# A hybrid mLSTM, attention and MLP layer on one core: another grouping of one weight preparation, block sums of the second MLP product made earlier, some stores on another queue

## The chip, the cores and the metric

The kernel runs on one core of a Trainium2 chip. The metric is the device time of one execution in microseconds (us). Its five engines are named as in the profile: PE (TensorE, matmuls; PEld is its weight load), DVE (VectorE), ACT (ScalarE), POOL (GpSimd) and SP (SyncE, which here does nothing but issue DMAs). Each engine works through its own list of instructions in order; an engine that waits at one instruction holds back all that stand behind it in its list.

## The reference

One layer, sequence 1024, width 1024, all in float32:

```
u    = rms_norm(h, norm1_g);  proj = u @ w_in
h    = h + concat(mlstm_mixer(proj...), neighbourhood_attention(proj...)) @ w_out
z    = rms_norm(h, norm2_g) @ w_ff1                 # 1024 x 4096
h    = h + square(relu(z)) @ w_ff2                  # 4096 x 1024
gate = sigmoid(rms_norm(h, ple_norm_g) @ w_ple_gate)
h    = h + gate * (p @ w_ple_up)
```

The change touches the third and fourth line alone, the MLP with its squared ReLU.

## The kernel before, in words

A float32 product is made of three passes: each operand x is split into a rounded part xh (ACT copies x into the type fp32r) and a rest xl = x - xh (DVE subtracts), and PE adds ah·bh, ah·bl and al·bh into one PSUM bank. So every block of weights costs an ACT copy, then a DVE subtraction, before PE can finish with it; in tile names the last letter, h or l, is that part. One matmul is 128x128 by 128x512.

**First MLP product (w_ff1).** The 4096 hidden columns are 16 groups of 256. Groups 2 to 15 are done by the Strassen-Winograd scheme, seven products of blocks instead of eight. Its products are called by their weight operands: 11, 12, 21, 22 are blocks of the weights, and s1 = 21 + 22, s2 = s1 - 11, s3 = 11 - 21, s4 = 12 - s2 are sums of them. `prep(c)` (with `put`) loads a group's weights, makes the sums and splits them into four pairs of tiles called a (11, 12), b (s2, s4), c (s3, 22) and d (s1); these tiles come from one ring with two buffers, so that c takes over the buffer of a, and d that of b, when PE has read it for the last time. The activations' sums (bt and the like) are made by `sum_blocks`. Group 2 is the first of its kind: `first_prods` runs its products while the activations' sums are still being made, with s2, s3 and 22 interleaved and s1 last. Groups 0 and 1 are plain products (p0a, p1a and, later, p0b, p1b), split in halves of which the first stand before group 2 and the second behind group 15.

While group 2 is on PE, `squares` sums h² over the width for the norm: ACT squares a 128x512 half (sq), POOL adds it to Rb; 14 adds, with two buffers for sq, so that the third square has to wait for the first add, and so on.

**The planes of z.** `relu2` and `z_blocks` make the squared ReLU's Winograd sums of a group's output and `z_put` stores them to DRAM as zd[0] to zd[3]; four halves go by SP's queue (`PQ`), the others by ACT's.

**Second MLP product (w_ff2).** `ff2_sweep` runs four sweeps, i = 2, 0, 1, 3, each with its own operands. A step of sweeps 2, 0 and 1 handles one group c with 24 matmuls (f_P): it needs zh and zl (the plane zr loaded and split, `zload`) and two blocks of w_ff2 (`w2_blocks`). In sweep 0 these blocks are sums: `w2_blocks(0, c)` loads ev (named w2re) and od (w2ro), 512 KB each, makes four sums (two on DVE, two on POOL), keeps two of them (sk) for sweep 1, and splits the other two, half by half, into w2h and w2l. `nadd` is how many of the former sweep's results are added to h (h<-h,evP) in a step.

**Order.** What stands ahead on an engine is set by the program's order and by `issue_after`, which ties a load to an earlier instruction; a step's loads and splits are issued some instructions ahead of its matmuls.

Of the kernel before, what the change touches and what calls it, by code (L numbers as in the profile page):

```python
# [18 lines left out]
P = 128  # L19
# [40 lines left out]
def tile_block(ctx, tc, xT, pT, w_in, w_out, w_ff1, w_ff2, w_gate, w_up, vecs, gate_b, rpbp, con,  # L60
# [95 lines left out]
    def wview(w, k0, k1, c0, c1):  # L156
        return w[k0 * P : k1 * P, c0:c1].rearrange("(k p) n -> p k n", p=P)
# [764 lines left out]
    with tc.tile_pool(name="m2", bufs=2) as m2, tc.tile_pool(name="m2p", bufs=2, space=PSUM) as m2p:  # L922
# [269 lines left out]
    with tc.tile_pool(name="ff1", bufs=1) as ff1:  # L1192
# [62 lines left out]
        def plain(nm, w, B1_, B2_, order, z):  # L1255
# [9 lines left out]
            for f in range(len(w)):  # L1265
                S.activation(z[f], pss[f], AF.Copy)

        def first_prods(nm, w, z):

            c11, c12, c21, u2 = z[0][:, 0:512], z[0][:, 512:], z[1][:, 0:512], z[1][:, 512:]  # L1270
            names = (("11", "11"), ("12", "21"), ("s4", "22"), ("s2", "t2"), ("s3", "t3"), ("22", "t4"), ("s1", "t1"))
            ps = {an: ps_(f"{nm}_{an}_{bn}") for an, bn in names}

            def part(an, bn, j):
                for i, (x_, y_) in enumerate(passes(w[an][0][:, j], w[an][1][:, j], *B[bn, j])):
                    TE.matmul(ps[an], x_, y_, start=j == 0 and i == 0, stop=j == 3 and i == 2)
# [16 lines left out]
            add(c12, c12, ps["s1"])  # L1293
            add(u2, u2, ps["s1"])
# [13 lines left out]
        def w2raw(i, c, rows, e0, e1, pool, tag, bufs):  # L1308
            raw = pool.tile([P, T], F32, tag=tag, name=f"w2r{i}_{c}", bufs=bufs)
            n = e1 - e0  # L1310
            for s, f in enumerate(rows):
                nc.sync.dma_start(raw[:, s * n : (s + 1) * n], w_ff2[f * P : (f + 1) * P, e0:e1])
            return raw

        def w2_blocks(i, c):

            wr = wp, "wr", 3
            if i == 0:
                ev = w2raw("e", c, (2 * c,), 0, D, ff2, "gh", 4)
                od = w2raw("o", c, (2 * c + 1,), 0, D, ff2, "gl", 4)  # L1320
                a11, a21, a12, a22 = ev[:, 0:512], ev[:, 512:], od[:, 0:512], od[:, 512:]
                sk[c] = utile32(f"sk{c}")
                s1, s3 = sk[c][:, 0:512], sk[c][:, 512:]
                V.tensor_tensor(s1, a21, a22, op=ALU.add)
                V.tensor_tensor(s3, a11, a21, op=ALU.subtract)  # L1325
                G.tensor_tensor(a21, s1, a11, op=ALU.subtract)  # L1326
                G.tensor_tensor(a22, a12, a21, op=ALU.subtract)
                hl = wp.tile([P, T], F32R, tag="wh", name=f"w2h0_{c}"), wp.tile([P, T], F32R, tag="wl", name=f"w2l0_{c}")
                for s, src in enumerate((a22, a21)):
                    ss = slice(s * 512, (s + 1) * 512)  # L1330
                    S.activation(hl[0][:, ss], src, AF.Copy)
                    V.tensor_tensor(hl[1][:, ss], src, hl[0][:, ss].bitcast(F32), op=ALU.subtract)
# [82 lines left out]
        wp1 = [plain_w("w1p", f, (utile(f"w1ph{f}"), utile(f"w1pl{f}"))) for f in (2, 3)]  # L1415
        sum_blocks(2)
        first_half(1, wp1)
        with after("t1"):
            w = prep(2)
        sum_blocks(3)  # L1420
        zt[2] = utile32("z2_0"), utile32("z2_1")
        first_prods("p2", w, zt[2])
# [53 lines left out]


    with tc.tile_pool(name="ff2", bufs=2) as ff2:
        acc3 = {}


# [58 lines left out]
        def g_split(j, t=None):  # L1540

            if j not in GH:
                GH[j] = (ff2.tile([P, T], F32R, tag="gh", name=f"gh{j}", bufs=4) if j < 4 else utile(f"gh{j}")), utile(f"gl{j}")
            hs = slice(0, T) if t is None else slice(t * 512, (t + 1) * 512)
            hi, lo = (t_[:, hs] for t_ in GH[j])
            g = vcol(V_G3, j)
            S.activation(hi, hres[j][:, hs], AF.Copy, scale=g)
            V.scalar_tensor_tensor(lo, hres[j][:, hs], g, hi.bitcast(F32), op0=ALU.mult, op1=ALU.subtract)
# [156 lines left out]
```

## Time and profile before

| | |
|---|---|
| time, median of 3 runs (lowest to highest) | 1400.39 us (1400.2 to 1402.23) |
| the profiled execution's own time | 1407.04 us |
| its span | 1405.3 us |
| PE busy | 1330.1 us, 95%, 7139 matmuls |
| PEld busy | 1109.6 us, 79% |
| DVE busy | 903.2 us, 64% |
| ACT busy | 598.5 us, 43% |
| POOL busy | 513.6 us, 37% |
| DMA | 211.27 MB, 150 GB/s in the mean |

PE is busy nearly throughout, so what can be won lies where it stops, or runs at less than its full clock. The share of the whole span tells little of that: a stop is read from the stage in which it stands. A line of a timeline gives the start, the duration, the engine, the line, out<-in, the shape, how many alike are merged, and in brackets how long the engine was idle before and who released it. Ends of matmuls are modelled, so their starts are what to compare.

### The profile page before, as it was taken

To read this page: it belongs to the slowest core of one execution; us is meant where nothing else is said; L and a number is where in the kernel's file an instruction comes from. 1 tells how busy PE (TensorE), PEld (TensorE's weight loads), DVE (VectorE), ACT (ScalarE), POOL (GpSimd) and SP (SyncE) were. 2 spreads that over 40 slices of the span, in tenths; PEclk is the share of its full clock that TensorE was granted. 3 is DMA by queue.
4 is the path that set the end of the run, shared out by engine and by line. 5 is a ranking of instruction groups with operands and counts; after the bars stand their busy time and mean duration, and the time that the engine had idled before them with its cause. 6 is when DMAs were issued, how large, how long until landed. Compare 5 with 4: busy or idle time off the path is not lost.

```text
span 1405.3 us, 19398 instructions
## 1 busy us (share of the span) xinstructions
PE 1330.1 (95%) x7139; PEld 1109.6 (79%) x7139; DVE 903.2 (64%) x1419; ACT 598.5 (43%) x985; POOL 513.6 (37%) x409
## 2 busy tenths in 40 slices
PE   7999999999998889999799999998999899999998
PEld 5988778799896667777587778886888678888887
DVE  4487786665672555667666666665448998559543
ACT  7353433364553545535433333334344234455321
POOL 2215675463321111100527665563302561007422
PEclk9999999999998899999899999999999999999999
DMA  8543333475323653313124644447786683542342
GB/s 291 197 147 96 107 108 106 169 228 165 109 65 102 177 162 126 105 61 103 45 85 163 220 155 149 145 135 239 268 300 212 196 254 102 167 148 74 106 142 83
DMA packets 158158, 211.27 MB, mean 150 GB/s; under 512 B 17904, under 2 KB 106992, under 8 KB 158064
## 3 DMA queue, kind: packets, MB, share of 16 engines
q1 hardware_dynamic: 149968, 192.07, 42.9%
q10 hardware_dynamic: 6624, 12.06, 2.5%
q0 software_dynamic: 1472, 5.92, 1.3%
q8 instruction: 56, 0.92, 0.3%
q14 instruction: 38, 0.31, 0.1%
HBM read 155.79 MB, written 54.21 MB: 149 GB/s over the span
## 4 chain that ended last, share of the span: by engine, by line
PE 56%; DVE 5%; DMA 5%; POOL 3%; issue 3%; ACT 2%; SPq 0%; DVEq 0%; POOLq 0%; ACTq 0%
PE f_P L1508 18%; PE op L1025 6%; PE p_s_t L256 6%; PE g L1577 6%; PE p L256 4%; PE p_s L256 2%; PE p_t L256 2%; DMA nr<-qnd 2%; PE pv L997 1%; PE pt L977 1%; PE o1p L312 1%; DMA tab<-tabI 1%; POOL Rb L1247 1%; PE p1a L1263 1%; PE sc L947 1%
## 5 line engine op out<-in xcount | busy, mean ns | idle before, releaser
L1345 DVE TENSOR_TENSOR zl<-zr,zh 128x1024 fp32r<-128x1024 f32 x56 | 81.9, 1470 | 20.1 <-ACT zh L1344 14.7
L966 POOL TENSOR_SCALAR pc<-pc,st 128x288 f32<-128x288 f32 (+1 forms) x32 | 17.4, 545 | 159.5 <-DVE st L961 124.8
L1344 ACT ACTIVATE zh<-zr 128x1024 fp32r<-128x1024 f32 x56 | 58.2, 1047 | 19.7 <-DMA zr<-zd 14.9
L1326 POOL TENSOR_TENSOR w2re<-sk,w2re 128x512 f32<-128x512 f32 x16 | 27.0, 1686 | 99.9 <-DVE sk L1325 85.2
L956 ACT ACTIVATE pc<-pc,st 128x288 f32<-128x288 f32 (+1 forms) x64 | 36.3, 569 | 56.0 <-DVE st L955 56.0
L1508 PE MATMUL f_P<-zl,w2h 128*128 128x512 f32 x128 | 52.3, 408 | 6.4 <-DVE zl L1345 6.4
L955 DVE CUSTOM_DVE_ANT_1 pc<-sc,tab 128x288 f32<-128x288 f32 (+1 forms) x64 | 29.9, 504 | 40.6 <-DMA tab<-tabU 22.0
L1508 PE MATMUL f_P<-zh,w2h 128*128 128x512 f32 x128 | 51.0, 398 | 1.1 <-ACT zh L1344 1.1
L1577 PE MATMUL g<-gh,wg_h 128*128 128x512 f32 (+1 forms) x136 | 51.8, 381 | 0.0
L1577 PE MATMUL g<-gl,wg_h 128*128 128x512 f32 (+1 forms) x136 | 51.3, 377 | 0.0
L1577 PE MATMUL g<-gh,wg_l 128*128 128x512 f32 (+1 forms) x136 | 51.2, 377 | 0.0
L1508 PE MATMUL f_P<-zh,w2l 128*128 128x512 f32 x128 | 51.1, 399 | 0.0
L790 POOL TENSOR_SCALAR wv<-vh,wj 128x129 f32<-128x129 f32 x56 | 30.4, 546 | 56.5 <-PE num L791 51.7
L1531 POOL TENSOR_TENSOR h<-h,evP 128x512 f32<-128x512 f32 x8 | 14.8, 1886 | 98.3 <-ACT evP L1522 98.3
L1372 POOL TENSOR_TENSOR tz<-z,z 128x512 f32<-128x512 f32 x14 | 19.4, 1388 | 73.2 <-ACT z L1358 73.1
L260 DVE TENSOR_TENSOR z<-z,p_s_t 128x512 f32<-128x512 f32 x52 | 34.5, 684 | 17.5 <-PE p_s_t L256 16.2
L1247 POOL TENSOR_TENSOR Rb<-Rb,sq 128x512 f32<-128x512 f32 x14 | 17.7, 1310 | 70.6 <-ACT sq L1245 70.6
L1357 DVE SCALAR_TENSOR_TENSOR z<-z,Rb 128x1024 f32<-128x1024 f32 x28 | 42.0, 1510 | 0.0
L997 PE MATMUL pv<-pT,vw 128*64 128x128 f32 (+1 forms) x384 | 32.2, 296 | 7.6 <-DVE pT L986 3.5
L1583 DVE TENSOR_TENSOR z<-g,Rb 128x512 f32<-128x512 f32 (+1 forms) x17 | 11.0, 658 | 43.4 <-PE g L1577 37.5
L138 ACT ACTIVATE w_bh<-w_0r 128x1024 fp32r<-128x1024 f32 x14 | 14.8, 1061 | 56.3 <-POOL w_0r L234 53.9
L138 ACT ACTIVATE w_ah<-w_0r 128x1024 fp32r<-128x1024 f32 x14 | 14.9, 1062 | 54.8 <-PE p_t L256 46.7
(840 smaller groups left out, 4782.9 us busy)
## 6 DMA issues: line engine op xcount, KB each, us to landing
zr<-zd SPq DMA_DIRECT2D x56, 512.0 KB
w2r<-w_ff SPq DMA_DIRECT2D x48, 256.0 KB
zd<-z ACTq DMA_DIRECT2D x42, 256.0 KB
zd<-tz SPq DMA_DIRECT2D x32, 256.0 KB
w2re<-w_ff SPq DMA_DIRECT2D x16, 512.0 KB
w2ro<-w_ff SPq DMA_DIRECT2D x16, 512.0 KB
w_0r<-w_ff SPq DMA_DIRECT2D x14, 512.0 KB
w_1r<-w_ff SPq DMA_DIRECT2D x14, 512.0 KB
```

The source lines that it names most:

```text
L256: TE.matmul(ps, x_, y_, start=j == 0 and i == 0, stop=j == 3 and i == 2)
L260: mark["add"] = V.tensor_tensor(o, a, b, op=ALU.add).ins
L790: G.tensor_scalar(wv, vh[:, c, 0:129], wj[:, col], 1.0, op0=ALU.mult, op1=ALU.mult)
L956: S.activation(pb, pb, AF.Exp, scale=-1.0, bias=st[:, 0:1], accum_out=st[:, 1:2])
L997: TE.matmul(pv[e0 : e0 + 64, cb], vws[pr][: 4 * kw, cb, rb + j, e0 : e0 + 64], pT[s][: 4 * kw, j], start=j == 0, stop=j == 2)
L1025: TE.matmul(ps, a, b, start=n == 0 and i == 0, stop=n == len(ks) - 1 and i == 2)
L1247: G.tensor_tensor(Rb[:, hs], Rb[:, hs], sq[:, hs], op=ALU.add)
L1344: S.activation(hi, raw, AF.Copy)
L1345: dv.append(V.tensor_tensor(lo, raw, hi.bitcast(F32), op=ALU.subtract).ins)
L1357: V.scalar_tensor_tensor(z_, z_, 0.0, Rb, op0=ALU.max, op1=ALU.mult)
L1508: pe_last = TE.matmul(ps[n, e], a, b, start=st and k == 0, stop=sp and k == 2)
L1577: TE.matmul(ps, x_, y_, start=k == 0 and i == 0, stop=k == KT - 1 and i == 2)
```

## The change

Three parts, all in the MLP.

1. `first_w()` takes the place of `prep(2)`. The same two loads, the same four sums; the blocks are grouped as a (11, 12), b (s4), c (s2, s3), d (22, s1), and each block is split by itself (512 columns). The tie of group 2's preparation to the activations' sums (`after("t1")`) goes.
2. `w2_load` and `w2_sums` take loads and sums out of `w2_blocks(0, c)`. All four sums are on DVE; they are made five groups ahead and the loads six (those of groups 0 to 4 during sweep 2, by the table `ahead`); two results overwrite the two halves of w2re, so that step c splits one tile of 1024 columns. w2re has six buffers and w2ro two, instead of four and four. Sweep 0's `nadd` is 1 instead of 2.
3. `z_put`: for c = 0, 1 and 15 the four stores of SP's queue are issued by POOL.

The diff, without the comment-free rest of `early`, whose tiles take buffers of the new rings:

```diff
+        def first_w():
+            raw = []
...
+            def put(x_, *parts):
+                hi, lo = (wp.tile([P, T], F32R, tag="w" + y_, name=f"w1_2_{x_}{y_}") for y_ in "hl")
+                for i, (an, src) in enumerate(parts):
+                    h_, l_ = hi[:, i * 512 : i * 512 + 512], lo[:, i * 512 : i * 512 + 512]
+                    S.activation(h_, src, AF.Copy)
+                    V.tensor_tensor(l_, src, h_.bitcast(F32), op=ALU.subtract)
+                    w[an] = [y_.rearrange("p (k n) -> p k n", n=P) for y_ in (h_, l_)]
+            put("a", ("11", a11), ("12", a12))
+            V.tensor_tensor(s1, a21, a22, op=ALU.add)
+            V.tensor_tensor(a21, a11, a21, op=ALU.subtract)
+            V.tensor_tensor(a11, s1, a11, op=ALU.subtract)
+            V.tensor_tensor(a12, a12, a11, op=ALU.subtract)
+            put("b", ("s4", a12))
+            put("c", ("s2", a11), ("s3", a21))
+            put("d", ("22", a22), ("s1", s1))
...
+        def w2_load(c):
+            w2eo[c] = w2raw("e", c, (2 * c,), 0, D, ff2p[0], "gh", 6), w2raw("o", c, (2 * c + 1,), 0, D, ff2p[0], "gl", 2)
+        def w2_sums(c):
+            ev, od = w2eo.pop(c)
...
+            V.tensor_tensor(s1, a21, a22, op=ALU.add)
+            V.tensor_tensor(s3, a11, a21, op=ALU.subtract)
+            V.tensor_tensor(a21, s1, a11, op=ALU.subtract)
+            V.tensor_tensor(a11, a12, a21, op=ALU.subtract)
+            skw[c] = ev
...
-                G.tensor_tensor(a21, s1, a11, op=ALU.subtract)
-                G.tensor_tensor(a22, a12, a21, op=ALU.subtract)
...
+                hl = split(wp, skw.pop(c), T, "w", f"w2_0_{c}")
+                for f_, c_ in ((w2_sums, c + 5), (w2_load, c + 6)):
+                    if c_ < NC_:
+                        f_(c_)
...
-            (PQ if (i, s) in ((0, 1), (1, 1), (1, 0), (3, 0)) else nc.scalar).dma_start(zd[i][:, c, s * 512 : (s + 1) * 512], src)
+            ((nc.gpsimd if c in (0, 1, NC_ - 1) else PQ) if (i, s) in ((0, 1), (1, 1), (1, 0), (3, 0)) else nc.scalar).dma_start(zd[i][:, c, s * 512 : (s + 1) * 512], src)
...
-        with after("t1"):
-            w = prep(2)
+        w = first_w()
...
+        ahead = {6 + 2 * c: [(w2_sums, c), (w2_load, c + 2)][: 2 if c < 4 else 1] for c in range(5)}
+        ahead[5] = [(w2_load, 0), (w2_load, 1)]
-        op, _ = ff2_sweep(2, 0, ("P2", "P1"), pre, {}, 0)
-        op, _ = ff2_sweep(0, 1, ("P3", "P6"), op, {}, 2)
+        op, _ = ff2_sweep(2, 0, ("P2", "P1"), pre, ahead, 0)
+        op, _ = ff2_sweep(0, 1, ("P3", "P6"), op, {}, 1)
```

PE's own order is that of before, but for the tiles that hold s2 and 22 of group 2. Where other engines' orders move, in three places:

ACT during group 2's products, before: the squares, then d (s1), then group 3's first weights.

```order
L1287 ACTIVATE z_1_6917<-p_11_11_6918 128x512
L1245 ACTIVATE sq_7042<-h_4888 128x512 x2
L1245 ACTIVATE sq_7042<-h_4943 128x512 x2
L1245 ACTIVATE sq_7042<-h_4998 128x512 x2
L1245 ACTIVATE sq_7042<-h_5137 128x512 x2
L1245 ACTIVATE sq_7042<-h_5196 128x512 x2
L1245 ACTIVATE sq_7042<-h_6546 128x512 x2
L138 ACTIVATE w_2_dh<-s_2_6874 128x512
L1245 ACTIVATE sq_7042<-h_6548 128x512
L138 ACTIVATE w_3_ah<-w_3_0r 128x1024
L1245 ACTIVATE sq_7042<-h_6548 128x512
```

The same place now (c is s2 and s3, d is 22 and s1):

```order
L1283 ACTIVATE w_2_ch<-w_2_0r 128x512
L1283 ACTIVATE w_2_ch<-w_2_1r 128x512
L1245 ACTIVATE sq_7048<-h_4888 128x512 x2
L1283 ACTIVATE w_2_dh<-w_2_1r 128x512
L1283 ACTIVATE w_2_dh<-s_2_6878 128x512
L1245 ACTIVATE sq_7048<-h_4943 128x512 x2
L1245 ACTIVATE sq_7048<-h_4998 128x512 x2
L1245 ACTIVATE sq_7048<-h_5137 128x512 x2
L1245 ACTIVATE sq_7048<-h_5196 128x512 x2
L1245 ACTIVATE sq_7048<-h_6546 128x512 x2
L1245 ACTIVATE sq_7048<-h_6548 128x512
L138 ACTIVATE w_3_ah<-w_3_0r 128x1024
```

Both copies of w_2_d have moved ahead of the squares that wait for POOL; w_3_ah stands where it stood, behind the last square but one.

SP's queue around the start of the second product (sweep 2's first two loads are zr_0 and zr_1; the four stores between them are group 15's), before:

```order
L1343 DMA zr_0_8973<-zd_108 128x1024
L1365 DMA zd_106<-tz_8963 128x512
L1365 DMA zd_107<-tz_8963 128x512
L1365 DMA zd_107<-z_0_8832 128x512
L1365 DMA zd_109<-z_1_8833 128x512
L1343 DMA zr_1_8986<-zd_108 128x1024
L1312 DMA w2r_2_9086<-w_ff 128x512
```

Now:

```order
L1382 DMA zr_0_8979<-zd_108 128x1024
L1341 DMA w2r_2_9092<-w_ff 128x512
L1382 DMA zr_1_8992<-zd_108 128x1024
L1474 DMA z0d<-zd_108 128x1024
L1341 DMA w2r_3_9258<-w_ff 128x512 x2
```

The four stores have left this queue for POOL's, and zr_1 follows zr_0 with one load between them.

DVE in sweep 0, about one step, before (w2l is the rest of the split weights, sk the sums kept, evP what is added to h):

```order
L1332 TENSOR_TENSOR w2l_2_9857<-w2ro_9849,w2h_2_9856 128x512
L1324 TENSOR_TENSOR sk_9898<-w2re_9894,w2ro_9896 128x512
L1345 TENSOR_TENSOR zl_2_9843<-zr_2_9841,zh_2_9842 128x1024
L1332 TENSOR_TENSOR w2l_2_9857<-w2re_9847,w2h_2_9856 128x512
L1325 TENSOR_TENSOR sk_9898<-w2re_9894 128x512
L1531 TENSOR_TENSOR h_4998<-h_4998,evP_3_9758 128x512
L1531 TENSOR_TENSOR h_6548<-h_6548,evP_3_9758 128x512
L1324 TENSOR_TENSOR sk_9945<-w2re_9941,w2ro_9943 128x512
L1325 TENSOR_TENSOR sk_9945<-w2re_9941 128x512
```

Now (w_0_2l and w_0_3l are the split weights of steps 2 and 3; the sums stand between them):

```order
L141 TENSOR_TENSOR w_0_2l<-w2re_9413,w_0_2h 128x1024
L1384 TENSOR_TENSOR zl_2_9892<-zr_2_9890,zh_2_9891 128x1024
L1356 TENSOR_TENSOR sk_9900<-w2re_9861,w2ro_9863 128x512
L1357 TENSOR_TENSOR sk_9900<-w2re_9861 128x512
L1570 TENSOR_TENSOR h_5196<-h_5196,evP_1_9807 128x512
L1358 TENSOR_TENSOR w2re_9861<-sk_9900,w2re_9861 128x512
L1570 TENSOR_TENSOR h_4943<-h_4943,evP_2_9809 128x512
L1359 TENSOR_TENSOR w2re_9861<-w2ro_9863,w2re_9861 128x512
L141 TENSOR_TENSOR w_0_3l<-w2re_9496,w_0_3h 128x1024
```

The two sums that POOL made (w2re<-sk,w2re and w2re<-w2ro,w2re) are now DVE's, among the adds to h; the split is one subtraction of 1024 columns, and the sums in a step belong to a group five steps later.

## Rows read from the trace of the kernel before

**Rows 1.** PE's waits from 640 us: us in total, times, longest
```profile
PE f_P L1508 <- DVE zl L1345: 6.4, 4, 1.9
PE p_s_t L1276 <- ACT w_dh L138: 5.7, 1, 5.7
PE f_P L1508 <- ACT zh L1344: 5.2, 3, 2.1
PE p_s_t L1276 <- DVE w_dl L141: 3.0, 1, 3.0
...
PE p1a L1263 <- ACT w1ph L138: 1.0, 1, 1.0
```

**Rows 2.** Windows: busy us (instructions) by engine, PEclk, DMA share, GB/s
```profile
690.00:706.00 16.00, 7.53 (x18) 5.49 (x19) 8.80 (x8) 5.13 (x8) 9.09 (x8) 0.57 0.00 0
1104.00:1145.00 41.00, 36.48 (x153) 28.47 (x153) 41.00 (x39) 12.60 (x18) 24.41 (x14) 0.99 0.72 227
997.00:1083.00 86.00, 86.00 (x381) 71.28 (x380) 50.16 (x46) 34.55 (x39) 16.89 (x10) 1.00 0.75 260
1015.00:1035.00 20.00, 20.00 (x90) 16.59 (x89) 9.09 (x8) 6.59 (x7) 0.00 (x0) 1.00 1.03 399
```

**Rows 3.** Timeline of PE, 688:707: start, us, operation, [idle before]
```profile
689.30 0.39 PE L1276 MATMUL p_t<-bth,w_cl 128*128 128x512 f32 x1
695.42 1.22 PE L1276 MATMUL p_s_t<-bt,w_dh 128*128 128x512 f32 x2 [5.73 <-ACT w_dh L138]
699.69 0.80 PE L1276 MATMUL p_s_t<-bt,w_dl 128*128 128x512 f32 x1 [3.04 <-DVE w_dl L141]
...
704.12 1.06 PE L256 MATMUL p<-b,w_ah 128*128 128x512 f32 x2
...
705.94 0.39 PE L256 MATMUL p<-b,w_al 128*128 128x512 f32 x1
```

**Rows 4.** Timeline of ACT, 680 to 706 us
```profile
680.68 1.14 ACT L1245 ACTIVATE sq<-h 128x512 f32<-128x512 f32 x2
...
694.76 0.61 ACT L138 ACTIVATE w_dh<-s 128x512 fp32r<-128x512 f32 x1
...
695.98 1.04 ACT L138 ACTIVATE w_ah<-w_0r 128x1024 fp32r<-128x1024 f32 x1
```

**Rows 5.** Timeline of POOL, 678 to 706 us
```profile
681.38 17.70 POOL L1247 TENSOR_TENSOR Rb<-Rb,sq 128x512 f32<-128x512 f32 x14 [70.63 <-ACT sq L1245]
```

**Rows 6.** Timeline of DVE, 680 to 706 us
```profile
695.40 4.23 DVE L141 TENSOR_TENSOR w_dl<-s,w_dh 128x512 fp32r<-128x512 f32 x1 [5.62 <-ACT w_dh L138]
...
700.16 1.21 DVE L141 TENSOR_TENSOR w_al<-w_0r,w_ah 128x1024 fp32r<-128x1024 f32 x1
```

**Rows 7.** Timeline of PE, 966 to 986 us
```profile
975.18 1.64 PE L1508 MATMUL f_P<-zh,w_0h 128*128 128x512 f32 x3 [2.03 <-ACT zh L1344]
...
981.17 0.96 PE L1508 MATMUL f_P<-zh,w_1h 128*128 128x512 f32 x3 [2.06 <-ACT zh L1344]
```

**Rows 8.** Timeline of SP's queue, 966 to 986 us
```profile
968.92 0.38 SPq L1343 DMA_DIRECT2D zr<-zd  x1
...
972.80 1.77 SPq L1365 DMA_DIRECT2D zd<-z  x2
974.66 0.40 SPq L1343 DMA_DIRECT2D zr<-zd  x1
```

**Rows 9.** Timeline of PE, first matmuls of sweep 0 and after it
```profile
1078.82 0.39 PE L1508 MATMUL f_P<-zh,w2h 128*128 128x512 f32 x1
...
1179.53 0.39 PE L1508 MATMUL f_P<-zh,w_0h 128*128 128x512 f32 x1
```

**Rows 10.** Timeline of DVE, 1112 to 1128 us, in sweep 0
```profile
1123.59 1.78 DVE L1324 TENSOR_TENSOR sk<-w2re,w2ro 128x512 f32<-128x512 f32 x1
1125.30 0.68 DVE L1325 TENSOR_TENSOR sk<-w2re 128x512 f32<-128x512 f32 x1
...
1126.50 2.31 DVE L1345 TENSOR_TENSOR zl<-zr,zh 128x1024 fp32r<-128x1024 f32 x1
```

More of the change, by code (lines that the diff above doesn't have):

```diff
@@ L1266, in plain @@
                 S.activation(z[f], pss[f], AF.Copy)
+        def first_w():
+            raw = []
+            for f in range(2):
+                r = wp.tile([P, T], F32, tag="wr", name=f"w1_2_{f}r", bufs=3)
+                nc.sync.dma_start(r.rearrange("p (k n) -> p k n", n=P), wview(w_ff1, 0, 8, (4 + f) * P, (5 + f) * P))
+                raw.append(r)
+            a11, a12, a21, a22 = raw[0][:, 0:512], raw[0][:, 512:], raw[1][:, 0:512], raw[1][:, 512:]
+            s1 = ff1.tile([P, 512], F32, tag="s1", name="s1_2")
+            w = {}
+            def put(x_, *parts):
[13 more added lines that the diff above has]
+            put("d", ("22", a22), ("s1", s1))
+            return w
         def first_prods(nm, w, z):
@@ L1313, in w2raw @@
             return raw
+        skw, w2eo = {}, {}
+        def w2_load(c):
+            w2eo[c] = w2raw("e", c, (2 * c,), 0, D, ff2p[0], "gh", 6), w2raw("o", c, (2 * c + 1,), 0, D, ff2p[0], "gl", 2)
+        def w2_sums(c):
+            ev, od = w2eo.pop(c)
+            a11, a21, a12, a22 = ev[:, 0:512], ev[:, 512:], od[:, 0:512], od[:, 512:]
+            sk[c] = utile32(f"sk{c}")
+            s1, s3 = sk[c][:, 0:512], sk[c][:, 512:]
+            V.tensor_tensor(s1, a21, a22, op=ALU.add)
[3 more added lines that the diff above has]
+            skw[c] = ev
+        ff2p = []
         def w2_blocks(i, c):
@@ L1318, in w2_blocks @@
             if i == 0:
[L1319 to L1325, printed above, removed]
-                G.tensor_tensor(a21, s1, a11, op=ALU.subtract)
-                G.tensor_tensor(a22, a12, a21, op=ALU.subtract)
[L1328 to L1332, printed above, removed]
+                hl = split(wp, skw.pop(c), T, "w", f"w2_0_{c}")
+                for f_, c_ in ((w2_sums, c + 5), (w2_load, c + 6)):
+                    if c_ < NC_:
+                        f_(c_)
                 return hl
@@ L1478, in tile_block @@
     with tc.tile_pool(name="ff2", bufs=2) as ff2:
+        ff2p.append(ff2)
         acc3 = {}
@@ L1542, in g_split @@
             if j not in GH:
-                GH[j] = (ff2.tile([P, T], F32R, tag="gh", name=f"gh{j}", bufs=4) if j < 4 else utile(f"gh{j}")), utile(f"gl{j}")
+                GH[j] = (ff2.tile([P, T], F32R, tag="gh", name=f"gh{j}", bufs=6) if j < 4 else utile(f"gh{j}")), utile(f"gl{j}")
             hs = slice(0, T) if t is None else slice(t * 512, (t + 1) * 512)
@@ L1587, in g_out @@
             nc.sync.dma_start(outT[e * P : (e + 1) * P, cs], hres[e][:, cs])
-        op, _ = ff2_sweep(2, 0, ("P2", "P1"), pre, {}, 0)
-        op, _ = ff2_sweep(0, 1, ("P3", "P6"), op, {}, 2)
+        ahead = {6 + 2 * c: [(w2_sums, c), (w2_load, c + 2)][: 2 if c < 4 else 1] for c in range(5)}
+        ahead[5] = [(w2_load, 0), (w2_load, 1)]
+        op, _ = ff2_sweep(2, 0, ("P2", "P1"), pre, ahead, 0)
+        op, _ = ff2_sweep(0, 1, ("P3", "P6"), op, {}, 1)
         early3, u_tile = [], utile
         def early(c):
-            utile = u_tile if c < 3 else lambda n: ff2.tile([P, T], F32R, tag="gl", name=n, bufs=4)
+            f2 = lambda tag, bufs: lambda n: ff2.tile([P, T], F32R, tag=tag, name=n, bufs=bufs)
+            zt_, wt_ = (u_tile, u_tile) if c < 3 else (f2("gl", 2), f2("gh", 6))
             with tc.issue_after(dv[-LAG]):
-                z = zsplit(ff2.tile([P, T], F32, tag="zr", name=f"zr3_{c}"), utile(f"zh3_{c}"), utile(f"zl3_{c}"),
+                z = zsplit(ff2.tile([P, T], F32, tag="zr", name=f"zr3_{c}"), zt_(f"zh3_{c}"), zt_(f"zl3_{c}"),
                            zd[3][:, 2 * c : 2 * c + 2].rearrange("p c t -> p (c t)"))
                 raw = w2raw(3, c, (4 * c + 1, 4 * c + 3), 512, D, wp, "wr", 3)
-                early3.append((z, split(wp, raw, T, "w", f"w2_3_{c}", hl=(utile(f"w2_3_{c}h"), utile(f"w2_3_{c}l")))))
+                early3.append((z, split(wp, raw, T, "w", f"w2_3_{c}", hl=(wt_(f"w2_3_{c}h"), wt_(f"w2_3_{c}l")))))
         op, _ = ff2_sweep(1, 3, ("P5", "P7"), op, {EC + ES * c: [(early, c)] for c in range(NE)}, 1)
```

## The prediction

> **What bounds the kernel now.** I read the page's busy shares first: PE is busy for 95% of the span, so no engine but PE matters except where PE waits or runs at a lower clock. Then the list of PE's waits from 640 us on, the part that the change touches [rows 1]: the reader is to see that four of its lines belong to the places that the change edits. The stop for w_dh and w_dl (5.7 and 3.0 us) is at the end of group 2's products; the waits for zl and zh (6.4 and 5.2 us) are at the start of sweep 2 and in sweep 0. Third, the windows for what a full-speed stretch looks like [rows 2]: from 997 to 1083 us PE is busy all of 86.00 us with 381 recorded matmuls, 0.226 us each. Against that measure I count what each place loses, in matmul starts.
>
> Group 2 [rows 3]: from 689.30 to 705.94 us, 16.64 us, PE starts 18 matmuls (the merged rows counted out), which take 4.07 us at 0.226. So 12.6 us are lost: 8.8 by the two stops and 3.8 because the matmuls from 699.69 on come every 0.43 us until about 705.4. The granted clock of 690 to 706 us is 0.57 in the mean, where 1.00 is the 2.4 GHz level and half of it 1.2 GHz [rows 2]; it stayed low for some 5.7 us after work had resumed.
>
> Sweep 2's start [rows 7]: two stops, 2.03 and 2.06 us, each with a stretch of 0.43-us matmuls behind it.
>
> Sweep 0 [rows 9]: from 1078.82 to 1179.53 us, 100.71 us, for 16 steps of 24 matmuls; 384 at 0.226 are 86.8. Lost: 13.9 us. DVE is busy for 41.00 of 41.00 us from 1104 to 1145 us, and POOL for 24.41 beside it [rows 2].
>
> **Part 1, group 2's weights.** Removed: d, the tile of s1, waits no longer for the buffer that s2 held to the end of the interleaved products, and its copy no longer stands behind twelve squares. Those are paced by POOL: 14 adds take 17.70 us [rows 5], 1.26 each, and with two buffers ACT can square only as fast as POOL adds; w_dh came at 694.76 for that reason [rows 4]. Added: three more instructions on ACT and three on DVE, since blocks of 512 columns stand where pairs of 1024 stood; the elements are the same, and each product of 12 matmuls, 2.7 us, covers the split of the next. The first group also needs half of w_ah only before PE's p1a weights: I give 0.5 of the 1.0 us of p1a's wait [rows 1], -0.5.
>
> What is late next is group 3. Its w_ah stands where it stood, behind the thirteenth square, and comes at about 696.0 to 697.0 as before [rows 4], while PE would be through with s1 at 689.5 + 12 x 0.226 = 692.3. And w_al needs DVE. The trace shows what that costs beside POOL's adds: w_dl, 128x512 with both inputs in SBUF, was released at 695.40 and took 4.23 us, to the end of POOL's last add at 699.1 [rows 5, 6]; the 1024-wide w_al took 1.21 behind it [rows 6]. So POOL's back-to-back adds keep such a DVE instruction out altogether. By this w_3_al goes from 699.1 to 700.3, PE's third matmul of group 3 starts there instead of at 704.98 or so, and the low clock follows the stop instead of preceding it: with 0.43 us per matmul to about 706 some 13 more are through by then, where before six were through at 706. Ten matmuls at 0.226 less: -2 us out of the 12.6.
>
> The same starvation decides the other end. In the new order w_2_dl (22 and s1) also falls beside the adds. PE's interleaved products are 36 matmuls, so they begin 8.1 us before 689.5, at 681.4, and the first of 22 comes after eight: PE needs its rest at about 683.2 us. Between the second and third square ACT now has the two copies of w_2_dh, 0.61 each [rows 4], so that the third add may have to wait for its square, and DVE can slip in there; if not, it waits to the end of the chain. My bounds for part 1 are therefore -12.6 (all of it) and +6 (rival 1). I take -2 - 0.5, nearest to the row of 4.23 us for w_3_al and to a DVE that gets in once.
>
> The Trainium skill ("SBUF — State Buffer", section "SBUF: two separate sides") says that DVE's instruction with two SBUF inputs and POOL's share a port pair as an exclusive lock, whichever starts first holding it for its whole instruction. The row of 4.23 us agrees that the loser stands still, but it stood still through three adds and not one. By the page's wording alone w_3_al would start one add after its release; that is rival 2.
>
> **Part 2, sweep 0's sums.** Removed: 32 POOL instructions of the sums, and one of the two instructions of each split. Added: 32 sums on DVE. A sum costs DVE 0.60 us where nothing disturbs it (the starts at 1125.30 and 1126.50 have two 512-wide instructions between them) and 1.78 where POOL is in the way; zl takes 2.31 in the same stretch [rows 10], against 1.21 for an undisturbed one of its size [rows 6]. Per step DVE has the rest of the weights 1.14, zl 1.14, four sums 2.40 and one add 0.60: 5.28 us, for the steps whose sums remain (0 to 10), against PE's 24 x 0.226 = 5.42. That fits by 0.14 us, once POOL is silent, and since the sums belong to a group five steps later, it is the order on DVE alone that can hold up a step. Some of the first steps carry two adds (5.88 us). I leave 3.4 us of the 13.9 as lost to that: -10.5. Bounds: -13.9, and 0 if DVE is as late as before.
>
> In sweep 2 five groups' sums come in: 5 x 2.40 = 12 us, and DVE has 86.00 - 50.16 = 35.8 us free there [rows 2], so their cover is large. Their loads are 1 MB a group, six groups by the table, in a sweep whose DMA share is 0.75 (260 GB/s); 1015 to 1035 us shows 399 GB/s with PE busy all 20.00 us [rows 2]. In sweep 0 a step loads 1.5 MB in 5.42 us, 277 GB/s, below that too. A sum that waits for its load stands in front of the next zl on DVE; the price is 0 to +3 us, and I take 0.
>
> **Part 3, the stores.** SP issued zr_0 at 968.92, then held four stores back until their data was made, and issued zr_1 at 974.66 [rows 8]; PE got it at 981.17, 6.5 us later, having waited 2.06 [rows 7]. Now zr_1 follows with one 0.4-us issue between, at about 969.8. With the 6.5 us of before PE has it at 976.3; allowing two us for the two loads beside each other, at 978.3, and it needs it at 979.1. So the second stop goes, 2.06 us, with its low-clock matmuls: about nine at 0.43 instead of 0.226 (estimate from the count between 981 and 985 us), 1.7 us. Sum -3.7, bounds 0 and -4.5. The first stop remains: zr_0 is issued when it was. POOL takes over twelve issues, behind its own sums, and waits for no one there.
>
> The Trainium skill ("DMA: Bandwidth & Descriptors", section "Issuing engines are not separate DMA queues") says that all issuers use the same 16 DMA engines and that another issuer only saves the issue time. Here that is the point: the row shows an issue held 5.7 us by its neighbours, not a slow transfer. By that rule the stores and zr_1 would still meet, which is the two us allowed above.
>
> **Sum.** -2 - 0.5 - 10.5 + 0 - 3.7 = -16.7 us against the profiled execution's 1407.04 us, which is 6.65 above the median of the runs; against 1400.39 that gives 1383.7, and I say 1384.
>
> **Rivals.**
> 1. DVE is kept out at group 2. If w_2_dl finds no gap, it waits from 682 to 699.1; PE stops at 683.2 with 40 matmuls of group 2 before it. From 699.3 on, 13 at 0.43 and 27 at 0.226 take 11.7, so that group 3 begins at 711 instead of 704.12: about +6 after the low-clock tail of before is taken off. Total -16.7 + 2 + 6 = -8.7: 1392. For it speaks the 4.23-us row, against it the gap behind the second square. Chance 0.2.
> 2. The port is given up after one add: w_3_al runs at 697.0 to 698.2, w_2_dl loses 1 us, and group 2 gains 4.5 to 8; if w_3_ah, too, comes sooner, up to 12.6. With sweep 0 as forecast: 1374 to 1381, say 1378. For it speaks that no row shows the new sequence; against it the 4.23 us. Chance 0.2.
> 3. Slower: DVE becomes the bound of the second product. The place is steps 1 to 10 of sweep 0, the price what a step exceeds 5.42 us. It decides when ACT's copies or the loads of w2ro, which has two buffers instead of four, keep DVE idle for over 1.5 us a step in order: then a step takes 6.8 and 10 steps lose what was won, and with part of the steps of sweep 2 losing alike (16 x 0.5), and rival 1 beside it, it comes to 1404 to 1410. For it speaks the margin of 0.14 us; against it that sums lie five groups ahead, so that a late load has 27 us to arrive. Chance 0.08.
> 4. Sweep 0 doesn't do what it should: its stops stay, because the loads and not DVE's load end them; then parts 1 and 3 alone, 1394 to 1400. For it speaks SP's queue, whose loads still wait for DVE's buffers; against it DVE's 41.00 of 41.00 us. Chance 0.1.
>
> The forecast keeps 0.42. A difference under 0.2%, 2.8 us, is not told from none. Faster: 0.42 + 0.2 + 0.2 and most of the last, 0.86; same 0.06; slower 0.08. The range runs from rival 2's middle to past rival 1: 1374 to 1396; the forecast's own is 1380 to 1388.
>
> **What would show it.** Right: no PE stop at w_2_d, one of some us before group 3's w_al, w_3_al ending with POOL's last add; one stop instead of two at sweep 2's start; 16 steps of sweep 0 in 87 to 91 us, DVE near 97% in its first ten, sums at 0.68 us. Wrong: a PE stop of over 10 us at 683 us (rival 1), sweep 0 steps of over 5.6 us with DVE busy (rival 3) or idle before a load (rival 4).

## The result, and the profile after

The changed kernel takes 1384.39 us (median of 4 runs, 1381.68 to 1386.4) against 1401.31 us for before: the ratio is 0.9877, with a 95% interval of 0.9854 to 0.9899, so it is 1.2% faster. The profiled execution took 1383.18 us, its span is 1381.4. The forecast was 1384.

PE's waits from 640 us on, to be read against [rows 1] (engine, line, what was waited for, us in total, times, longest):

```profile
PE p L256 <- ACT w_ah L138: 5.7, 1, 5.7
PE f_P L1547 <- ACT zh L1383: 2.6, 1, 2.6
PE p L256 <- DVE w_al L141: 2.4, 4, 0.8
...
PE p1a L1263 <- ACT w1ph L138: 0.6, 1, 0.6
...
PE f_P L1547 <- DVE w_4l L141: 0.4, 1, 0.4
PE f_P L1547 <- DVE zl L1384: 0.3, 1, 0.3
```

The stops for zl and zh in sweep 0 are gone. The stop of 5.7 us for group 2's w_dh is gone as well, but one of 5.7 us stands in the list for group 3's w_ah, which was not there before. PE's timeline shows where, as in [rows 3]:

```profile
686.51 0.39 PE L1305 MATMUL p_s_t<-bt,w_dl 128*128 128x512 f32 x1
692.58 1.22 PE L256 MATMUL p<-b,w_ah 128*128 128x512 f32 x2 [5.68 <-ACT w_ah L138]
694.51 0.80 PE L256 MATMUL p<-b,w_al 128*128 128x512 f32 x1 [0.71 <-DVE w_al L141]
...
698.50 0.40 PE L256 MATMUL p<-b,w_al 128*128 128x512 f32 x1
```

Group 2 now ends without a stop, and PE stops one product later, with a stretch of low clock behind it as before: from 695.11 us on the matmuls come every 0.43 us until about 698.3, and the granted clock of 686.6 to 698.5 us is 0.71 in the mean. The windows of sweep 0 (busy us and instructions of PE, PEld, DVE, ACT, POOL, then PEclk, DMA share, GB/s), its first 41.6 us and the whole, against [rows 2]:

```profile
1068.40:1110.00 41.60, 41.60 (x185) 34.47 (x184) 41.14 (x56) 16.58 (x18) 0.00 (x0) 1.00 0.78 264
1068.40:1155.50 87.10, 87.10 (x386) 72.12 (x385) 73.21 (x93) 34.39 (x38) 0.00 (x0) 1.00 0.61 201
```

PE is busy in all of it at full clock, POOL not at all, and DVE is nearly as full in the first half as it was before (99% against 41.00 of 41.00 us), but with undisturbed instructions.

Where the time went, by the starts of the matmuls with the same number in the profiles (us). "Again" are second profiles of the same two kernels; a stage ends where the next begins.

| stage | before | before again | after | after again |
|---|---|---|---|---|
| up to the out projection's end, not changed | 631.58 | 632.66 | 628.11 | 627.59 |
| groups 0, 1 and 2, to early in group 3 | 83.92 | 82.14 | 79.03 | 79.32 |
| of these, from p1a's middle on | 48.41 | 48.25 | 45.56 | 45.85 |
| groups 3 to 15 | 244.98 | 244.90 | 244.48 | 244.47 |
| to the end of sweep 2 | 118.34 | 121.00 | 116.79 | 117.34 |
| sweep 0 | 100.71 | 101.14 | 87.06 | 87.04 |
| sweeps 1 and 3, gate | 220.73 | 220.76 | 220.72 | 220.74 |

The two first profiles are 24 us apart, the medians 17. Of that 7 us, 3.5 lie in the stage that the change doesn't touch. The rest lies in stages that it does touch: those shrink by 20.6 us between the first profiles and by 21.0 between the second ones. Both profiled executions of before (1407.04 and 1409.39 us) took longer than the others in their runs (1399 to 1403), so a difference of two profiles is larger here than what the change is worth.

The line "early in group 3" has a flaw: where group 2 is prepared by `prep(2)`, four short matmuls of the norm stand before it, otherwise none. From p1a's middle to the first matmul of group 4, which has the same matmuls on both sides, it is 59.41 and 59.25 us before and 56.10 and 56.38 after: -3.1 and not -2.6.

### The profile page after: what moved, and what is told of

The parts are those of the page before. It is cut to its first block, busy times and chain, and to the rows that moved or that the text cites. A ratio compares the mean times of both kernels' runs of the same rounds, so it can differ in the third digit from the quotient of the medians.

```text
span 1381.4 us, 19321 instructions
## 1 busy us (share of the span) xinstructions
PE 1318.9 (95%) x7139; PEld 1103.6 (80%) x7139; DVE 895.0 (65%) x1438; ACT 597.3 (43%) x972; POOL 463.8 (34%) x389
## 4 chain that ended last, share of the span: by engine, by line
PE 60%; DMA 5%; DVE 4%; POOL 2%; ACT 2%; issue 1%; SPq 1%; DVEq 0%; ACTq 0%; POOLq 0%
PE f_P L1547 21%; PE op L1025 6%; PE p_s_t L256 6%; PE g L1616 6%; PE p L256 4%; PE p_s L256 2%; PE p_t L256 2%; DMA nr<-qnd 2%; PE pv L997 2%; PE pt L977 1%; POOL Rb L1247 1%; PE o1p L312 1%; DMA tab<-tabU 1%; PE sc L947 1%; DVE z L260 1%
## 5 line engine op out<-in xcount | busy, mean ns | idle before, releaser
L1384 DVE TENSOR_TENSOR zl<-zr,zh 128x1024 fp32r<-128x1024 f32 x56 | 71.4, 1280 | 20.7 <-ACT zh L1383 20.7
L1247 POOL TENSOR_TENSOR Rb<-Rb,sq 128x512 f32<-128x512 f32 x14 | 20.5, 1503 | 67.8 <-ACT sq L1245 67.8
L256 PE MATMUL p<-b,w_ah 128*128 128x512 f32 x104 | 34.1, 410 | 5.8 <-ACT w_ah L138 5.7
L138 ACT ACTIVATE w_bh<-w_0r 128x1024 fp32r<-128x1024 f32 x13 | 13.8, 1062 | 59.3 <-POOL w_0r L234 53.9
L1397 ACT ACTIVATE z<-z 128x1024 f32<-128x1024 f32 x28 | 29.6, 1058 | 14.9 <-DVE z L1396 14.2
L256 PE MATMUL q<-uh,wq_al 128*128 128x512 f32 x64 | 29.1, 455 | 7.1 <-DVE wq_al L141 7.1
L138 ACT ACTIVATE w_ah<-w_0r 128x1024 fp32r<-128x1024 f32 x13 | 13.8, 1061 | 51.0 <-PE p_t L256 47.3
L997 PEld LDWEIGHTS pv<-pT,vw 128*64 128x64 f32 (+1 forms) x384 | 22.8, 144 | 15.4 <-issue 7.7
```

Source lines behind the costliest of these rows:

```text
L256: TE.matmul(ps, x_, y_, start=j == 0 and i == 0, stop=j == 3 and i == 2)
L997: TE.matmul(pv[e0 : e0 + 64, cb], vws[pr][: 4 * kw, cb, rb + j, e0 : e0 + 64], pT[s][: 4 * kw, j], start=j == 0, stop=j == 2)
L1247: G.tensor_tensor(Rb[:, hs], Rb[:, hs], sq[:, hs], op=ALU.add)
L1384: dv.append(V.tensor_tensor(lo, raw, hi.bitcast(F32), op=ALU.subtract).ins)
```

## The experiments

### Each part undone

Four kernels on one chip; the changed kernel as it is was the base.

> The changed kernel as it is, beside the others on one chip, as their base. Every theory expects 1384.4 us, within the 1381.7 to 1386.4 us of its first runs, 0.988 of before. If the 24.1 us that lie between the two profiled executions were the change's, the ratio would be 0.983; the theory that 3.5 us of them are the profiled execution of before being late in a stage that the change doesn't touch expects 0.985 to 0.988.

Measured: 1383.61 us (1380.88 to 1389.04), ratio to before 0.9874 (0.9848 to 0.9899).

**Part 1 undone.**

```diff
-        w = first_w()
+        with after("t1"):
+            w = prep(2)
```

> The changed kernel with part 1 undone: group 2 prepared by prep(2) again, parts 2 and 3 kept. Theory A, that the terms read from the two traces add up: +5.4 us against the changed kernel (2.0 at p1a, 3.4 at group 2), 1389.8 us, with PE's stop of 5.7 us for w_dh back. Theory B, the prediction's own term: +2.5, 1386.9. Theory C, that group 3's stop swallows nearly all of it in every execution: +1 at most.

Measured: 1385.31 us, +1.7, ratio to before 0.988 (0.9856 to 0.9904), which overlaps the base's interval, so theories B and C are not told apart. Of theory A's two terms, the 3.4 us at group 2 fall by the profile. The waits of this kernel in 660 to 710 us, and its DVE instruction that answers to the one of 4.23 us in [rows 6]:

```profile
PE p_s_t L1305 <- ACT w_dh L138: 5.7, 1, 5.7
PE p_s_t L1305 <- DVE w_dl L141: 0.6, 1, 0.6
```

```profile
693.34 1.79 DVE L141 TENSOR_TENSOR w_dl<-s,w_dh 128x512 fp32r<-128x512 f32 x1 [5.62 <-ACT w_dh L138]
```

With the order of before, the stop of 5.7 us is back, but the second one is 0.6 us and not 3.0, since w_dl waited for one POOL add. From p1a's middle to the first matmul of group 4 this kernel takes 56.58 us, the changed one 56.10 and 56.38: the regrouping gives some tenths there (up to the table's line, 45.59 and 45.56). The other difference lies at p1a: 35.49 against 33.47 us from the out projection's end to p1a's middle.

**Part 2 undone** (the sums in the step, two on POOL, two adds a step):

```diff
-                hl = split(wp, skw.pop(c), T, "w", f"w2_0_{c}")
-                for f_, c_ in ((w2_sums, c + 5), (w2_load, c + 6)):
...
+                G.tensor_tensor(a21, s1, a11, op=ALU.subtract)
+                G.tensor_tensor(a22, a12, a21, op=ALU.subtract)
...
```

> The changed kernel with part 2 undone: sweep 0's sums in the step itself, two of four on POOL, two adds to h a step, four and four buffers; parts 1 and 3 kept. Theory A: +12.4 us (13.65 in sweep 0, less the 1.3 that sweep 2 gives back), 1396.8, with PE's waits for zl and zh in sweep 0 back. Theory B, the prediction's own term: +10.5, 1394.9.

Measured: 1395.64 us, +12.0, ratio to before 0.9955 (0.9941 to 0.997), as theory A has it; 1.5 us more than the prediction's term. Sweep 0 takes 100.81 us; its waits:

```profile
PE f_P L1536 <- DVE zl L1374: 7.3, 5, 2.4
PE f_P L1536 <- ACT zh L1373: 1.2, 1, 1.2
```

But the stage before it, to the end of sweep 2, takes 114.83 us, 2 us less than in the changed kernel.

**Part 3 undone.**

```diff
-            ((nc.gpsimd if c in (0, 1, NC_ - 1) else PQ) if (i, s) in ...
+            (PQ if (i, s) in ...
```

> The changed kernel with part 3 undone: the twelve stores on SP's queue again, parts 1 and 2 kept. Theory A, an issue held by its neighbours: +2.9 us, 1387.3, with the second stop at sweep 2's start (about 2 us) back. Rival, that stores and loads meet on the same DMA engines whoever issues them: no difference, 1384.4, and the stop is not there.

Measured: 1388.99 us, +5.4, ratio to before 0.9913 (0.9888 to 0.9939). The rival falls: the stops are there, in 960 to 1075 us:

```profile
PE f_P L1547 <- ACT zh L1383: 4.2, 2, 2.4
PE f_P L1547 <- DVE zl L1384: 2.5, 2, 2.2
```

It is larger than expected, as step 5 of sweep 2 stops for zl too (2.2 us). That stop is in neither profile of before: it needs the sums ahead as well (see "Two smaller questions"), so the parts don't simply add. The three differences, 1.7 + 12.0 + 5.4 = 19.1 us, come near the 18.4 us between base and before on this chip.

The later kernels ran on two other chips, without the base beside them; before took 1401.47 and 1401.14 us there, against 1401.97 here, so their differences to the base are uncertain by some 0.8 us more.

### What about the sums made sweep 0 fast

**Two sums back on POOL, still ahead.**

```diff
-            V.tensor_tensor(a21, s1, a11, op=ALU.subtract)
-            V.tensor_tensor(a11, a12, a21, op=ALU.subtract)
+            G.tensor_tensor(a21, s1, a11, op=ALU.subtract)
+            G.tensor_tensor(a11, a12, a21, op=ALU.subtract)
```

> The changed kernel with two of the four sums of sweep 0's weights given back to POOL, still five groups ahead. It tells contention from lateness as the cause of sweep 0's stops before. If DVE's instructions being held up by POOL's was the cause: zl takes 2.3 us again in places, DVE is near 100% busy in sweep 0, PE stops come back, +4 to +12 us against the changed kernel (1388 to 1396). If it was only that the sums were made in the step that used them: no stop in sweep 0, within 1 us of 1384.

Measured: 1400.89 us, ratio to before 0.9993 (0.9979 to 1.0007): all of the gain is gone, more than the bound given. Its window of sweep 0, its waits there and two places on DVE:

```profile
1072.90:1175.50 102.60, 91.83 (x385) 73.79 (x384) 75.53 (x73) 34.51 (x37) 33.77 (x20) 0.97 0.51 171
```

```profile
PE f_P L1547 <- DVE zl L1384: 10.6, 5, 3.4
```

```profile
1092.21 4.08 DVE L1570 TENSOR_TENSOR h<-h,evP 128x512 f32<-128x512 f32 x3
...
1098.55 2.29 DVE L1384 TENSOR_TENSOR zl<-zr,zh 128x1024 fp32r<-128x1024 f32 x1
```

Three adds take 4.08 us, where three undisturbed ones take 1.88 (at 1084.43 us of before), and zl behind them is late. But DVE is busy for 75.53 of 102.60 us, not near 100%, as was expected: here the order on DVE is another (adds in threes and fives), and SP's loads of w2ro, with two buffers, wait for POOL's last sum. The run mixes contention with a queue, and the stops part into the two. Ahead of the first two (1.74 and 3.41 us) DVE never rests: it is busy for 36.00 of the 36.10 us up to 1109. Ahead of the other three (5.5 us in total) it had waited 1.9 to 3.1 us for a load of w2re. So lateness of the sums alone was not the cause, but only the first two stops speak for contention.

**All sums on DVE and nothing else**, from the kernel before:

```diff
-                G.tensor_tensor(a21, s1, a11, op=ALU.subtract)
-                G.tensor_tensor(a22, a12, a21, op=ALU.subtract)
+                V.tensor_tensor(a21, s1, a11, op=ALU.subtract)
+                V.tensor_tensor(a22, a12, a21, op=ALU.subtract)
```

> The kernel before with all four sums on DVE and nothing else changed: the sums in the step that uses them, two adds to h a step. If contention with POOL was the cause, most of the 13.9 us lost in sweep 0 come back, -8 to -12 us against before (1389 to 1393), though two adds a step make 5.9 us on DVE against PE's 5.42 for eight steps (up to +3.8). If lateness was the cause: stops stay or grow, 1400 or more.

Measured: 1387.08 us, ratio to before 0.9894 (0.9876 to 0.9911), -14.4, better than the bound. The window of sweep 0:

```profile
1072.60:1160.10 87.50, 87.45 (x386) 71.94 (x386) 81.36 (x120) 36.87 (x52) 0.00 (x0) 1.00 0.69 233
```

Two lines of code, with the sums in the step that uses them, four and four buffers and two adds a step, give nearly all of sweep 0's gain: 87.45 us, 13.3 less than before. Another 2.6 us of this profile lie at group 2, where w_dl was held for one add only (last section); no line of the edit touches that place. This shows that POOL's part in the sums was the cause, and that neither the lead of five groups nor the new buffers are needed for it. Whether POOL held DVE up or was only slow itself, the edit can't tell; the rows of before can, for part of it. Ahead of the last three of its five stops (4.5 of 7.5 us, 1114 to 1129 us) DVE was never idle, with instructions of 1.78 and 2.31 us in place of 0.68 and 1.21. The first two (3.0 us) came behind two sums of POOL, the first of them itself held up (an undisturbed one takes 1.28 us), and DVE stood idle for the copy of the result:

```profile
1089.94 3.48 POOL L1326 TENSOR_TENSOR w2re<-sk,w2re 128x512 f32<-128x512 f32 x1 [13.05 <-DVE sk L1325]
```

```profile
1095.48 1.08 DVE L1332 TENSOR_TENSOR w2l<-w2ro,w2h 128x512 fp32r<-128x512 f32 x1 [3.21 <-ACT w2h L1331]
```

Whether sums of undisturbed length would have been in time there is not shown.

### The stop ahead of group 3

**Squares in two lots**: four rows as now, four tied behind w_3_ah on ACT.

```diff
...
             with after("lo"):
-                squares()
+                squares(range(4))
+            with after("lo", "ahi"):
+                squares(range(4, KT))
```

> The changed kernel with the squares of the last four of eight rows tied behind group 3's first weight copy on ACT; all the work is the same. If w_3_ah's place behind thirteen POOL-paced squares sets the stop of 5.7 us ahead of group 3, the copy runs when PE gives its buffer free, at about 684 us of the changed kernel's profile, PE stops for under 1 us, and the low clock behind it goes too: -7 to -9 us, 1375 to 1377. Rival, that the norm's statistics become late (the last adds end as late as now, some 696 us, and PE uses them at 709.6): the same time, with a stop at the norm's matmuls.

Measured: 1381.98 us, ratio to before 0.9843 (0.9822 to 0.9864), -1.6 against the base. Neither theory holds. Its waits in 660 to 720 us:

```profile
PE p_s_t L257 <- ACT w_bh L138: 3.4, 1, 3.4
PE p_s_t L257 <- DVE w_bl L141: 0.7, 1, 0.7
```

The stop ahead of w_3_ah is gone, and the next copy, w_3_bh, which now stood behind all the squares, made one of its own. Hence the next run.

**The adds on DVE.**

```diff
-                        G.tensor_tensor(Rb[:, hs], Rb[:, hs], sq[:, hs], op=ALU.add)
+                        V.tensor_tensor(Rb[:, hs], Rb[:, hs], sq[:, hs], op=ALU.add)
```

> The changed kernel with the squares' fourteen adds on DVE instead of POOL; the order then puts all squares but the first two behind group 3's weights. No two-input instruction of DVE meets a POOL add there. If POOL's pace alone made the stop, PE runs into group 3 with under 1 us of stop: -7 to -9 us. Rival: the squares now come so late that the norm's matmuls at 709.6 us wait for them, fourteen squares at 0.63 us from about 700 us on: a stop of 1 to 3 us there and a gain of 4 to 7 us.

Measured: 1389.7 us, ratio to before 0.9901 (0.9883 to 0.9919), +6.1 against the base. The rival named the right wait and had its size wrong:

```profile
PE n2ps L167 <- DVE Rb L1247: 8.8, 1, 8.8
```

Groups 2 and 3 run without a stop of a us (69.74 us in the table's second stage), and the norm's matmuls then wait 8.8 us for squares that the order had put behind the weights.

**Squares in three lots**: four rows, two behind w_3_ah, two behind w_3_bh.

```diff
...
-                squares()
+                squares(range(4))
+            with after("lo", "ahi"):
+                squares(range(4, 6))
+            with after("lo", "bhi"):
+                squares(range(6, KT))
```

> The changed kernel with the squares in three lots on ACT: four rows as now, two behind group 3's copy w_3_ah, two behind w_3_bh (before, with two lots, the stop of 5.7 us ahead of w_3_ah went and one of 3.4 us ahead of w_3_bh came). If the place behind POOL-paced squares is all that makes these copies late, both stops go: PE stops under 1.5 us in group 3, -7 to -9 us against the changed kernel in the profile's stage, 1375 to 1377. If the sums that w_3_bh needs (on DVE, beside POOL's adds) are late themselves, a stop of 1 to 3 us stays there and the time is 1378 to 1381.

Measured: 1376.37 us, ratio to before 0.9815 (0.9796 to 0.9834), -7.2 against the base. The second stage takes 70.23 us instead of 79.0, 8.8 less. So the place of ACT's copies behind squares that POOL paces was the whole of that stop. In this profile 2.0 to 2.6 us of it were given back in the stage to the end of sweep 2 (119.35 us, against 116.79 and 117.34), by a stop of 1.9 us for zl in step 9; its waits from 950 us to the end of sweep 2:

```profile
PE f_P L1557 <- DVE zl L1390: 2.2, 2, 1.9
PE f_P L1557 <- ACT zh L1389: 2.0, 1, 2.0
```

**Combined**: parts 1 and 3, squares in three lots, all sums on DVE in the step, one add a step.

> The kernel before with part 1, part 3, the squares in three lots, one add to h a step in sweep 0, and all four sums on DVE in the step that uses them, not ahead. Theory: being ahead gives nothing and costs 1.4 us in sweep 2 through DVE waiting for loads, so this is 1 to 2 us faster than the run with squares in three lots: 1373 to 1376, sweep 0 without stops and sweep 2 too. Rival: being ahead hides the loads' waits in sweep 0; then stops of 2 us and more come there, 1377 or more.

Measured: 1373.09 us (1372.39 to 1373.66), ratio to before 0.9799 (0.9783 to 0.9814): the fastest median of all, 10.5 us below the base, though its interval overlaps that of squares in three lots. Sweep 0 has no stop, as the theory said; sweep 2 keeps its first stop and two of some tenths:

```profile
PE f_P L1546 <- ACT zh L1379: 2.7, 2, 2.0
PE f_P L1546 <- DVE zl L1380: 0.3, 1, 0.3
```

The stage to the end of sweep 2 takes 114.43 us and sweep 0 87.04.

### Two smaller questions

**Group 15's stores alone on POOL.**

```diff
-            ((nc.gpsimd if c in (0, 1, NC_ - 1) else PQ) if ...
+            ((nc.gpsimd if c == NC_ - 1 else PQ) if ...
```

> The changed kernel with group 15's stores alone on POOL; groups 0's and 1's are on SP's queue again. With all twelve on SP the time was 5.4 us longer, 1.5 us of it at the first two loads and 2.7 in the steps after them by its profile. If it is the queue's head that counts at each place: the first part stays won, the second is lost again, +2.5 to +3.5 us, 1386 to 1387, with a wait for zl in steps 3 to 5 of sweep 2. If the first two loads are all that counts: 1384.

Measured: 1385.25 us, ratio to before 0.9885 (0.9869 to 0.9901), +1.6 against the base, whose interval it overlaps. The stage to the end of sweep 2 takes 118.27 us, against 116.79 and 117.34 in the changed kernel and 121.18 with all twelve on SP. By the time, most of part 3 is group 15's four stores. The wait for zl that was expected came back, in step 5 (2.02 us at 1010.94), behind a DVE that waited for a load of the sums ahead:

```profile
PE f_P L1547 <- DVE zl L1384: 2.6, 3, 2.0
```

```profile
1003.98 0.69 DVE L1357 TENSOR_TENSOR sk<-w2re 128x512 f32<-128x512 f32 x1 [4.04 <-DMA w2re<-w_ff]
```

SP issued this stretch's loads of w2re from 998.20 us on, behind four stores of group 1 that it held back until 996.39; in the changed kernel the first of them went at 985.88. In before, before again and sums on DVE, which have these stores on SP's queue but no sums ahead, the stop isn't there. So what moving the other eight stores mends, by these rows, is a stop that part 2 would have brought.

**The kernel before again.**

> The kernel before once more, for a second profile: whether w_dl of group 2 is held through three POOL adds again. In the first profile it took 4.23 us, in two other kernels with the same order there 1.79 (one add). If that is an accident of one execution: 1.79 us, a second stop of 0.6 us instead of 3.0 and a span near 1400. If it is the order: 4.23 again and 3.0 us.

Measured: 1402.29 us, ratio 0.9997 (0.9978 to 1.0015). The instruction in question:

```profile
694.88 4.24 DVE L141 TENSOR_TENSOR w_dl<-s,w_dh 128x512 fp32r<-128x512 f32 x1 [5.64 <-ACT w_dh L138]
```

It is no accident of one execution: 4.24 us again, and the second stop is 3.1 us. See the last section.

## Why the prediction came out right, step by step

**Part 1, group 2 (-2): the size is near, the reason is wrong.** The stage from p1a's middle took 48.4 and 48.3 us before and 45.6 and 45.9 after, -2.6 (-3.1 by the first matmul of group 4). But the step that said why, w_3_al kept out until POOL's last add, failed. It waited for one add only and was through at 694.46 us, before POOL's last add (695.59); so did w_dl of s1, while 22's was not held at all:

```profile
676.50 0.73 DVE L1284 TENSOR_TENSOR w_dl<-w_1r,w_dh 128x512 fp32r<-128x512 f32 x1 [0.38 <-ACT w_dh L1283]
677.15 1.78 DVE L1284 TENSOR_TENSOR w_dl<-s,w_dh 128x512 fp32r<-128x512 f32 x1
...
692.56 1.90 DVE L141 TENSOR_TENSOR w_al<-w_0r,w_ah 128x1024 fp32r<-128x1024 f32 x1 [7.50 <-ACT w_ah L138]
```

What took its place is POOL's side of the same meeting. The adds, 17.70 us in [rows 5], were held up in turn:

```profile
675.06 20.54 POOL L1247 TENSOR_TENSOR Rb<-Rb,sq 128x512 f32<-128x512 f32 x14 [67.77 <-ACT sq L1245]
```

So w_3_ah, behind the thirteenth square, came later against the products, 15.6 us after the interleaved ones began (675.86 us) instead of 14.6, and made the stop alone (5.68 us; the stop for w_3_al is 0.71). This is why rival 2, which had the one-add wait right, had the time wrong (-4.5 to -8 there). The two kernels with prep(2) kept and w_dl at 1.79 us took 56.58 and 56.76 us from p1a's middle to group 4, against 59.41 and 59.25 in before: 2.7 of the 3.1 us are the difference between a DVE instruction held for one add and one held for three, and some tenths the regrouping's own. Rival 1 didn't come about. (The forecast's count to 706 us gives nine matmuls, not ten, which is -2 all the same.)

**p1a (-0.5).** The wait for w1ph went from 1.0 to 0.6 us, as said. Out projection to p1a's middle took 35.51 and 33.89 us before, 33.47 in both profiles after: in before's first profile the matmuls behind this stop come every 0.43 us until about 664.5, with a granted clock of 0.91 from 647.6 to 667.1 us, and in its second the clock is 1.00 there. So it is 0.4 to 2.0.

**Part 2, sweep 0 (-10.5): right mechanism, sized too small.** Measured 100.71 - 87.06 = 13.65 and, undone, 100.81 - 87.04 = 13.8. The 3.4 us set aside for DVE's order in the full steps were not lost: a margin of 0.14 us a step was enough. Rivals 3 and 4 fall with this.

**Part 2, sweep 2 (0, bound +3): it costs 1 to 2 us.** DVE waited there for a load in front of a split that PE needed, as the prediction priced it and then didn't count:

```profile
1000.29 0.69 DVE L1356 TENSOR_TENSOR sk<-w2re,w2ro 128x512 f32<-128x512 f32 x1 [3.22 <-DMA w2ro<-w_ff]
...
1001.63 1.22 DVE L141 TENSOR_TENSOR w_4l<-w2r,w_4h 128x1024 fp32r<-128x1024 f32 x1
```

To the end of sweep 2 the changed kernel took 116.79 and 117.34 us, the two kernels with its stores but without its sums ahead 114.83 and 114.43. Of that, by the matmuls' starts against 0.227 us each, 1.0 and 1.7 us are lost from w_4l on, behind these loads; the rest is at the sweep's first stop, which comes before the first sum.

**Part 3 (-3.7): right mechanism.** Undone, it costs 5.4 us, but part of that is the stop in step 5, which before doesn't have. SP now issues the two loads 1.1 us apart, with one other load between them (left out below), against 5.7 us in [rows 8]:

```profile
960.07 0.48 SPq L1382 DMA_DIRECT2D zr<-zd  x1
...
961.13 0.54 SPq L1382 DMA_DIRECT2D zr<-zd  x1
```

The second stop went, the first stayed (2.57 us), as said. What part 3 also does, keeping group 1's stores from holding back part 2's loads, had not been seen.

The mechanisms of parts 2 and 3 were right, that of part 1 at group 2 was not. That the sum fits to less than 1 us is partly luck. A term that was too small (sweep 0, by 3.2 us) and one left out (sweep 2, 1 to 2 us) have opposite signs; part 1 was paid by a wait of DVE that differs between kernels; and the terms were read from a profile 6.65 us slower than the median, but taken off the median. Between the profiles the touched stages gave 20.6 and 21.0 us, between the medians 16.9 here and 18.4 in the first experiment, against 16.7 forecast.

## What to carry to other kernels

Where DVE and POOL both work on SBUF beside a full PE, try the plainest cure first: give the shared work to one of them. Two lines of it were worth 13 us in sweep 0 here, and the lead of five groups nothing that the runs show; it needed another part of the change to mend what it brought. A stop that goes comes back at the next instruction of the same queue: look at what else stands behind the slow chain, and move the chain, not its first victim. And when one duration out of a single profile carries a term, look for the same instruction in a second kernel before trusting it.

## What was not expected of the hardware

The same DVE instruction, w_dl of s1 with the same neighbours on all three engines, released 0.04 to 0.07 us after a POOL add began, took 4.23 and 4.24 us in two profiles of before (three adds), and 1.79 us (one add) in two other kernels: part 1 undone (693.34 us) and sums on DVE (below), which differs from before only far behind this place.

```profile
691.22 1.79 DVE L141 TENSOR_TENSOR w_dl<-s,w_dh 128x512 fp32r<-128x512 f32 x1 [5.62 <-ACT w_dh L138]
```

The Trainium skill ("SBUF — State Buffer", section "SBUF: two separate sides") has the lock go to whichever starts first, for a whole instruction. That the loser stands still for a whole instruction agrees with these rows. But it need not be next when that instruction ends. In most places of all fourteen profiles a DVE instruction that was held ran after one POOL instruction. In before's two profiles w_dl ran after three; and in every profile, the changed kernel's and these two kernels' too, one far ahead of the change ran after two, 4.22 or 4.23 us against 1.21 undisturbed. In before:

```profile
196.47 2.38 POOL L496 TENSOR_TENSOR mqk<-mqk,zk 128x1024 f32<-128x1024 f32 x1
...
198.79 1.28 POOL L232 TENSOR_TENSOR wq_1r<-wq_0r,wq_1r 128x512 f32<-128x512 f32 x1
```

```profile
196.94 4.23 DVE L141 TENSOR_TENSOR wq_al<-wq_0r,wq_ah 128x1024 fp32r<-128x1024 f32 x1
```

For w_dl it repeats in the two profiles of before and differs between kernels; what in them decides it stays open.
